# Compressed keys of the NSA group in four column blocks of the array, and S5 products of two parities written alternately

## The chip, the cores and the metric

The kernel runs on one core of one Trainium2 chip. The metric is the time of one execution on the device in microseconds (us); the time before is the median of three runs. Engines are named as in the profile: PE is the matrix engine, PEld its weight load, DVE the vector engine, ACT the scalar engine, POOL GpSimd, SP the engine whose queue issues most of the transfers.

## The reference

Two layers of a hybrid decoder trunk for 256 tokens of width 2048, in f32. Each layer has a token-mixing block and a gated MLP of inner width 5632; both stand between two RMS norms and are shifted, scaled and gated by a vector that is computed from `c` (adaLN, a 2048 x 12288 product per layer). The mixing block projects the tokens once, hands the columns to four groups, and projects the joined results back:

```python
proj = h @ w_in
o_a = mla_mixer(...)    # multi-head latent attention, 4 heads
o_b = s5_mixer(...)     # diagonal complex state space model, 32 groups of 64 states
o_c = nsa_mixer(...)    # compressed, selected and windowed attention
o_d = gdn_mixer(...)    # gated delta rule, 4 heads, chunks of 64 tokens
o = concatenate([rms_norm(o_a), rms_norm(o_b), rms_norm(o_c), o_d])
return o @ w_out
```

Two pieces of it are touched by the change. In the NSA group the keys (and likewise the values) of overlapping blocks of 32 tokens, one block every 16 tokens, are flattened and sent through a small MLP:

```python
h = gelu((xb + pos_emb).reshape(B, N, 32 * 128) @ w1)    # 15 blocks, w1: 4096 x 128
return h @ w2
```

In S5 the input is mapped to complex states, scanned over time, and mapped back: `bu = u B`, `x_t = lam x_(t-1) + bu_t`, `y = Re(C x) + D u`, then gelu and a gated linear unit.

## The kernel before

**The stream.** All large products run on weights that pass once through the chip. A tile of 128 x 1024 f32 (512 KB) is loaded by SP's queue (`wload`), ACT rounds it to a first part `wh` (line 366), DVE subtracts to get the rest `wl` (line 367), and PE makes three products of the parts of weights and activations for each product wanted (`mm3`); their results lie in four PSUM tiles named `mm`. In the trace these are the products whose name begins with `mm<-`, here called the products of the stream; their operands are `ht` (activations) with `wh` or `wl`. The adaLN products of later blocks run in the background on tiles `rawa`, on DVE (line 412).

**The mixers.** Beside the stream stand the products of the groups. They are f32, and PE makes two passes for each, so that one product of the program shows as two records of the trace. Their results lie in PSUM tiles `mx`, in two pools `mx0` and `mx1` of two tiles each; `self.lane` says which of them a part of the program draws on, and `None` lets it draw on both in turn (lines 133 to 138). `mixers` (line 1423) issues in this order: S5 (on `mx0`), the narrow columns, the compression of the NSA keys and values (`nsa_compress`, on `mx1`), the two halves of GDN (two heads each; half 0 on `mx0`, half 1 on `mx1`), MLA (`mx0`), the NSA attention (`mx1`, later both), the output gate. `project_out` follows with the `w_out` weights.

**Who sets the order.** The program is issued once, and the framework's scheduler lays out from it, at build time, a fixed order of instructions for each engine, from dependences, buffers, priorities and its own estimates of time. On PE it puts the products of the groups between those of the stream. Each engine then runs its list in order. A part of a group that waits for another engine has products of the stream put before it, as long as there are any whose weights and PSUM tile are to be had: the stream's products are what PE does while a chain of small steps runs on ACT and DVE.

**NSA compression.** `st` holds the tokens by their place q in a stride of 16, `[128 features, 16, 18]`: 16 strides, and two columns for the position embedding. For each q one product of weights `st[:, q]` (18 columns) with 256 columns of `w1` is added to `acc[:18]`; `w1` comes in four transfers to tiles `rawm`, four q in each. `acc` is copied to `ab`, turned by two transposes (`tp`) to `psT`, and the small MLP goes on from there. All this happens twice per layer, for keys and values.

**S5.** Pairs of groups lie in eight quads; a pair has a parity `par`, which is the half of the 128 rows on which its input lies (rows 0 to 63 or 64 to 127). For each half of the quads and each parity, in turn: eight products V (64 rows deep, 128 columns, one PSUM tile for the real and one for the imaginary part), some twenty steps on DVE (rotate, scan, rotate back), then twelve products y, which write the 64 output partitions of the parity, then four gelus. The DVE steps leave the states in `t1`, `t2`, which the products y read. The tables of S5 (`s5_tables`, line 1280) are made in the time before; the products of its taps write 64 partitions of the output for either parity `e`.

**GDN and MLA.** A half of GDN begins on PE with the decay products (`mx<-tri,gg`), goes through normed keys to an inverse by blocks of 32 x 32, and ends with the state update over four chunks. MLA begins with two norms, and then its up-projections, `mx<-arena,rawm` 128x256.

Of the kernel before, what the change touches and what calls it, by code (L numbers as in the profile page):

```python
# [16 lines left out]
AF = mybir.ActivationFunctionType  # L17
# [26 lines left out]
RSC = -8192.0        # factor that rsqrt_cols leaves on its result  # L44

MBOOST = 300        # the same of the mixers' own weights
BOOST = 2500        # how far ahead of the arithmetic the weight stream is scheduled

# arena map (floats per partition)
A_KVT = 0                           # token-major narrow columns  # L50
A_SIL0 = A_KVT + 1704               # GDN inputs of heads 0, 1
A_GA = A_SIL0 + 1536                # S5, then GDN heads 0, 1, then MLA
A_SIL1 = A_GA + 6160                # S5 tables; GDN inputs of heads 2, 3
A_GB = A_SIL1 + 1536                # S5 tables; GDN heads 2, 3, then NSA
A_OT = A_GB + 7168                  # mixer outputs, feature-major
A_KEEP = A_OT + 4096                # compressed keys and values of the NSA group
NA = A_KEEP + 1024
A_X = A_KVT                         # the residual stream, but for the time of the mixers
A_Z = A_X + 4096                    # output of the mixing block before its norm
A_GP = A_SIL1                       # the output gate of the mixing block  # L60
FIRST = (O_U, O_U + 256, O_GQ)      # columns of the first products
A_TAB = A_SIL1                      # S5 tables, the rotations last
A_ROT = A_TAB + 4608
A_SCR, N_SCR = A_OT + 2048, 3072    # S5 tables being built
A_GPF = A_SCR                       # the output gate of the FFN
AT = [A_ROT + g * 1024 for g in range(4)] + [A_Z + g * 1024 for g in range(5)] + [A_OT, A_OT + 1024]   # the FFN's inner activations
ADA_DVE = (0, 2, 4, 6, 9, 11)       # tiles of a quarter that DVE multiplies
# [6 lines left out]
class Region:  # L74
    """Sequential carving of a range of the arena."""
# [16 lines left out]
class Ker:  # L92
    def __init__(self, ctx, tc, I, out):
# [5 lines left out]
        # operands in two parts of half the mantissa: h^T; then the mixer outputs, or the FFN's activations  # L99
# [11 lines left out]
        self.lane = None                # which of them the current group of instructions draws on; None: both in turn  # L111
# [4 lines left out]
        self.side = iter(())             # work between the tiles of the weight stream, one step at each  # L116
# [8 lines left out]
    # ---------------------------------------------------------------- helpers  # L125
# [20 lines left out]
    def rsqrt(self, v, y, a):  # L146
        """y = v ** -0.5; v and a are overwritten."""
# [9 lines left out]
    def rsqrt_cols(self, ss):  # L157
        """RSC * (ss / D + EPS) ** -0.5 of a few columns, in fewer dependent steps than rsqrt."""
# [26 lines left out]
    def sincos(self, ang, sin, cos, t):  # L185
        """sin and cos of ang; cos and t double as scratch."""
        nc = self.nc
        self.reduce_2pi(ang, cos, t)
        nc.scalar.activation(sin, cos, AF.Sin)
        nc.vector.scalar_tensor_tensor(t, cos, -1.0, cos, op0=ALU.mult, op1=ALU.max)  # L190
        nc.vector.tensor_scalar(t, t, -1.0, math.pi / 2, op0=ALU.mult, op1=ALU.add)
        nc.scalar.activation(cos, t, AF.Sin)

    # -------------------------------------------------------------- constants
    def constants(self):
# [39 lines left out]
        # compressed-block masks: valid where t >= 16 n + 31  # L235
# [26 lines left out]
    def condition(self):  # L262
        """silu(c), one column of 128 features each."""
# [12 lines left out]
    def vectors_ada(self, l, rg):  # L276
        """Per-feature vectors of the modulation, one column of 128 features each."""
# [10 lines left out]
    def vectors(self, l, rg):  # L288
        """Per-feature vectors of the rest."""
# [40 lines left out]
        # column 0: dt_bias, column 1: a_log  # L330
# [12 lines left out]
    # --------------------------------------------------------------- streams  # L343
    def wload(self, parts):
        """parts: list of (view of the raw tile, source AP); one raw tile of up to 1024 columns."""
# [18 lines left out]
    def split(self, src, hi, lo):  # L364
        """src in two parts of half the mantissa each, hi + lo."""
# [21 lines left out]
    def mm3(self, out, a, b, start, stop):  # L387
        """out (+)= a^T b with both in two parts."""
# [4 lines left out]
    def mload(self, parts):  # L393
        """Weights of the mixers, through a small ring of their own."""
# [6 lines left out]
    # ------------------------------------------------------------------ adaLN  # L401
# [24 lines left out]
        # the sum over partitions: within blocks of 32 by a transpose of the blocks, then over the four blocks  # L426
# [46 lines left out]
    def ada_out(self, l, b, cols, j=0):  # L473
        """Columns j and on of block b."""
# [18 lines left out]
    def gate_out(self, l, which):  # L493
        """gate * post-norm gain / RSC to DRAM, as one row."""
# [7 lines left out]
    def gate_rows(self, l, which):  # L502
        """That row, on all partitions."""
# [17 lines left out]
    def set_diag(self, ss):  # L521
        """diag takes the scale of the rows, from their sums of x^2, ss [128, 2]."""
# [6 lines left out]
    def pre_norm(self, l, which):  # L529
        """Fills h^T, 4 tiles of 4 chunks each; a generator that stops after each quarter of the features."""  # L530
# [27 lines left out]
    def norm_start(self, h):  # L558
        """Half of the features; the others along with the products."""
# [7 lines left out]
    def x_stats(self):  # L567
        """Row sums of x^2 [128, 2] from those of the blocks."""
# [8 lines left out]
    def post_block(self, ps, j, gp, sums, z, last, tts=(0, 1)):  # L577
        """One 512-column block of y (two PSUM tiles); z takes gate * y; sums the row sums of y^2, and of z^2 and 2 x z."""
# [15 lines left out]
    def residual(self, sums, zs, done):  # L594
        """x += r z, r the scale of the rows; the sums of the new x^2 as x^2 + r (2 x z + r z^2)."""
# [1132 lines left out]
```

## Time and profile before

| | us |
|---|---|
| median of three runs | 2695.22 (2687.34 to 2700.55) |
| span of the profiled execution | 2692.3 |
| left between that span and the median | 2.9 |

The trace is of one execution. A row with `xN` is N instructions in a row with the same form; the number behind the start is how long the whole run took, with the pipelined end of the last one, so the distance from a start to the next row's start is the better measure of what a run costs PE. `128*18 128x256` means weights of 128 rows and 18 columns, and 256 columns that stream past them on 128 rows. `[1.15 <-ACT arena L1280]` is idle time before a row and what ended it.

### The profile page before, as it was taken

What the parts mean: (1) busy time and instruction counts of PE and PEld (TensorE: products, weight loads), DVE (VectorE), ACT (ScalarE), POOL (GpSimd) and SP (SyncE); (2) the same over time, 40 slices, a digit from 0 to 9 for tenths busy, and PEclk for the clock granted to TensorE, in tenths of its full rate; (3) what the DMA queues carried; (4) which work ended last, traced back from release to release, by engine and by line L of the source; (5) the groups of instructions that cost most, each with busy time, mean ns of one, the idle gap of its engine ahead of it and who ended that gap; (6) DMA issues with size and microseconds to landing.
All of it is one profiled execution on the core that took longest, in us unless ns stands there. A gap on an engine that the chain in (4) does not pass through costs nothing. (4 is left out here: it accounts for less than half of the span.)

```text
span 2692.3 us, 44696 instructions
## 1 busy us (share of the span) xinstructions
PE 2553.3 (95%) x17587; PEld 2257.8 (84%) x17587; DVE 1924.8 (71%) x3036; ACT 1260.7 (47%) x2025; POOL 9.6 (0%) x21
## 2 busy tenths in 40 slices
PE   5899999798999999999998999999899999999998
PEld 2478788687999999988877879888799999998886
DVE  6668888778877777776878888865677655555555
ACT  4244554546545444444545445555544444444443
POOL 0000000000000000000000000000000000000000
PEclk7889999899999999999999999999999999999999
DMA  8986887676888888877776667835588766665554
GB/s 269 298 242 188 259 277 226 202 268 217 274 287 277 283 286 284 293 247 234 232 255 228 189 201 243 267 123 170 180 272 280 224 187 188 183 186 188 188 188 148
DMA packets 325899, 621.43 MB, mean 231 GB/s; under 512 B 45132, under 2 KB 131640, under 8 KB 324152
## 3 DMA queue, kind: packets, MB, share of 16 engines
q1 hardware_dynamic: 317632, 617.36, 71.5%
q8 instruction: 138, 2.26, 0.3%
q10 hardware_dynamic: 8056, 1.21, 0.3%
q14 instruction: 73, 0.60, 0.1%
HBM read 614.26 MB, written 4.23 MB: 230 GB/s over the span
## 5 line engine op out<-in xcount | busy, mean ns | idle before, releaser
L127 PE MATMUL mm<-ht,wh 128*128 128x256 f32 x7232 | 1311.4, 283 | 2.9 <-ACT wh L366 2.9
L366 ACT CAST wh<-raw 128x1024 fp32r<-128x1024 f32 (+1 forms) x740 | 771.2, 1043 | 953.8 <-PE mm L127 751.2
L367 DVE TENSOR_TENSOR wl<-raw,wh 128x1024 fp32r<-128x1024 f32 (+1 forms) x740 | 893.2, 1213 | 346.1 <-ACT wh L366 344.2
L127 PEld LDWEIGHTS mm<-ht,wh 128*128 128x128 f32 x7232 | 1114.1, 189 | 15.2 <-issue 6.8
L127 PE MATMUL mm<-ht,wl 128*128 128x256 f32 x3616 | 1023.9, 283 | 7.9 <-DVE wl L367 7.6
L127 PEld LDWEIGHTS mm<-ht,wl 128*128 128x128 f32 x3616 | 681.7, 189 | 20.2 <-DVE wl L367 12.8
L412 DVE SCALAR_TENSOR_TENSOR acc<-rawa,condc,acc 128x1024 f32<-128x1024 f32 x310 | 397.3, 1282 | 216.5 <-DMA rawa<-in_w_ada_dram 215.0
L127 PE MATMUL mm<-wh,ht 128*128 128x512 f32 (+1 forms) x1600 | 507.4, 395 | 3.4 <-ACT ht L366 2.9
L127 PEld LDWEIGHTS mm<-wh,ht 128*128 128x128 f32 x1600 | 300.9, 189 | 68.0 <-ACT ht L366 3.2
L127 PE MATMUL mm<-wl,ht 128*128 128x512 f32 (+1 forms) x800 | 316.1, 395 | 1.7 <-DVE wl L367 1.7
L127 PE MATMUL mx<-wh,ht 128*128 128x512 f32 x704 | 221.4, 395 | 0.0
L127 PE MATMUL mx<-arena 128*128 128x128 f32 (+8 forms) x1432 | 199.1, 280 | 12.5 <-ACT arena L1417 4.7
L127 PEld LDWEIGHTS mx<-arena 128*128 128x128 f32 (+5 forms) x1432 | 156.0, 170 | 51.4 <-issue 20.2
L127 PEld LDWEIGHTS mm<-wl,ht 128*128 128x128 f32 x800 | 151.6, 190 | 34.0 <-DVE wl L367 3.0
L127 PEld LDWEIGHTS mx<-wh,ht 128*128 128x128 f32 x704 | 132.0, 187 | 32.1
L127 PE MATMUL mx<-wl,ht 128*128 128x512 f32 x352 | 139.3, 396 | 0.9 <-DVE wl L367 0.8
L131 PE MATMUL mx<-ident,arena 128*128 128x128 f32 (+3 forms) x367 | 68.4, 290 | 32.4 <-ACT arena L1280 11.0
L367 DVE TENSOR_TENSOR ht<-arena,ht 128x1024 fp32r<-128x1024 f32 x52 | 63.6, 1223 | 39.4 <-ACT ht L366 39.0
L131 PEld LDWEIGHTS mx<-ident,arena 128*128 128x128 f32 (+3 forms) x367 | 44.4, 148 | 53.7 <-ACT arena L1280 12.7
L1557 DVE SCALAR_TENSOR_TENSOR arena<-mm,v,arena 128x255 f32<-128x255 f32 (+1 forms) x176 | 78.2, 476 | 4.3 <-ACT arena L1555 3.5
L127 PEld LDWEIGHTS mx<-wl,ht 128*128 128x128 f32 x352 | 66.0, 187 | 18.1 <-DVE wl L367 2.1
L366 ACT CAST ht<-arena 128x1024 fp32r<-128x1024 f32 x52 | 54.2, 1050 | 56.5 <-PE mm L127 32.3
(308 smaller groups left out, 1514.1 us busy)
## 6 DMA issues: line engine op xcount, KB each, us to landing
raw<-in_ffn_w_in_dram SPq DMA_DIRECT2D x352, 512.0 KB
rawa<-in_w_ada_dram SPq DMA_DIRECT2D x348, 512.0 KB
raw<-in_ffn_w_out_dram SPq DMA_DIRECT2D x176, 512.0 KB
raw<-in_w_in_dram SPq DMA_DIRECT2D x116, 512.0 KB
raw<-in_w_out_dram SPq DMA_DIRECT2D x64, 512.0 KB
rawm<-in_w_ada_dram SPq DMA_DIRECT2D x28, 512.0 KB
raw<-in_w_in_dram SPq DMA_DIRECT2D x16, 426.0 KB
raw<-in_w_in_dram SPq DMA_DIRECT2D x16, 354.0 KB
```

Of the source, the lines that this page charges most:

```text
L127: self.nc.tensor.matmul(out, lhsT=lhsT, rhs=rhs, start=start, stop=stop)
L131: self.nc.tensor.transpose(out, in_, self.ident[:k, :k])
L366: self.nc.scalar.copy(hi.bitcast(F32R), src)
L367: self.nc.vector.tensor_sub(lo.bitcast(F32R), src, hi)
L412: self.last_mac = self.nc.vector.scalar_tensor_tensor(acc, w, self.condc[:, kc:kc + 1], acc, op0=ALU.mult, op1=ALU.add)
L1557: nc.vector.scalar_tensor_tensor(c[:, s:], ps[m][:, :256 - s], self.fconv(l, 2 - s, f), c[:, s:], op0=ALU.mult, op1=ALU.add)
```

## The change

It has three parts.

1. `nsa_compress`: `st` has 32 columns for each q instead of 18, zeroed by POOL first. The four q of a `rawm` tile go to four blocks of 32 output partitions, `acc[32q : 32q + 32]`, each with its own sum over the four tiles. All 128 partitions are copied to `ab`. Instead of two transposes, four products with columns of `ident2` (two identities of 64, one above the other) turn `ab` and add the four blocks.
2. `s5_tables`: the loops over the parity `e` and over real and imaginary part are swapped.
3. `s5`: the products V of both parities come first, then the DVE steps of one parity and of the other, with a second pair of buffers `t1`, `t2` in the place of MLA's outputs, then the products y of both parities, written alternately. In `mixers`, S5 draws on all four `mx` tiles (`lane = None`).

```diff
-            st = r(16, 18)
+            st = r(16, 32)
+            nc.gpsimd.memset(st, 0.0)
...
-                    self.mm(acc[:18], st[:, q0 + q], raw[:, q * 256:(q + 1) * 256], q0 + q == 0, q0 + q == 15)
-            ab = r(256)[:18]
-            nc.scalar.copy(ab, acc[:18])
+                    self.mm(acc[32 * q:32 * q + 32], st[:, q0 + q], raw[:, q * 256:(q + 1) * 256], q0 == 0, q0 == 12)
+            ab = r(256)
+            nc.scalar.copy(ab, acc)
             psT = self.mx()
             for i in range(2):
-                self.tp(psT[:, i * 32:i * 32 + 18], ab[:, i * P:(i + 1) * P])
+                for j in range(2):
+                    self.mm(psT[:, i * 32:i * 32 + 32], ab[:, i * P:(i + 1) * P], self.ident2[:, 32 * j:32 * j + 32], j == 0, j == 1)
...
             for qd in range(4):
-                for e in range(2):
-                    for ri in range(2):
+                for ri in range(2):
+                    for e in range(2):
...
-        for qr in range(4):
-            half, par = qr // 2, qr % 2
+        for half in range(2):
             quads = range(4 * half, 4 * half + 4)
...
+            V = [[view(self.mx()) for _ in range(2)] for _ in range(2)]
             for ri in range(2):
-                ps = self.mx().rearrange("p (e n) -> p e n", e=4)
                 for e, qd in enumerate(quads):
-                    self.mm(ps[:, e], G[o:o + 64, qd, ri], Uc[o:o + 64, qd], True, True)
-                V.append(ps)
+                    for par in range(2):
+                        o = 64 * par
+                        self.mm(V[par][ri][:, e], G[o:o + 64, qd, ri], Uc[o:o + 64, qd], True, True)
...
+            y = [view(self.mx()) for _ in range(2)]
             for e, qd in enumerate(quads):
-                yy = y[o:o + 64, e]
-                self.mm(yy, To[o:o + 64, qd], Uc[o:o + 64, qd], True, False)
-                for ri, t in enumerate((t1, t2)):
-                    self.mm(yy, H[:, 2 * qd + par, ri], t[:, e, 0:P], False, ri == 1)
+                for par in range(2):
+                    o = 64 * par
+                    self.mm(y[par][o:o + 64, e], To[o:o + 64, qd], Uc[o:o + 64, qd], True, False)
+                for ri in range(2):
+                    for par in range(2):
+                        o = 64 * par
+                        self.mm(y[par][o:o + 64, e], H[:, 2 * qd + par, ri], ts[par][ri][:, e, 0:P], False, ri == 1)
...
+        self.lane = None
+        self.s5(l, r5, Uc, oT["s5"])
         self.lane = 0
-        self.s5(l, r5, Uc, oT["s5"])
```

The scheduler makes its order anew, and three places of PE's list in layer 0 show what comes of it. In each row the name left of the arrow is the tile written, with its number; the shape is that of the result, partitions by columns; `xN` is N products of the program in a row.

First the beginning of S5's first products V. Before, the tiles `mx0_1283` and `mx0_1288` are the real and imaginary part of parity 0:

```order
L127 MATMUL mx0_1283<-arena_58 128x128 x2
L127 MATMUL mx0_1288<-arena_58 128x128 x2
L127 MATMUL mm_1533<-wh_1540,ht_59 128x426
L127 MATMUL mx0_1283<-arena_58 128x128
L127 MATMUL mx0_1288<-arena_58 128x128
L127 MATMUL mm_1533<-wl_1541,ht_59 128x426
L127 MATMUL mm_1533<-wh_1540,ht_59 128x426 x2
```

In the changed kernel `mx1_1285` and `mx0_1286` belong to parity 0, `mx1_1287` and `mx0_1288` to parity 1:

```order
L127 MATMUL mx1_1285<-arena_58 128x128
L127 MATMUL mx1_1287<-arena_58 128x128
L127 MATMUL mx1_1285<-arena_58 128x128
L127 MATMUL mx1_1287<-arena_58 128x128
L127 MATMUL mx0_1286<-arena_58 128x128
L127 MATMUL mx1_1285<-arena_58 128x128
L127 MATMUL mx0_1288<-arena_58 128x128
L127 MATMUL mx0_1286<-arena_58 128x128
L127 MATMUL mx0_1288<-arena_58 128x128
L127 MATMUL mx0_1286<-arena_58 128x128
```

Products of the two parities, which use different rows of the array, now stand partly next to each other: four such pairs are in this piece, and 14 of the 32 that there could be in both layers. The others follow one of their own parity, or stand alone.

Second, the products y. Before, one parity's last ten of twelve:

```order
L127 MATMUL mm_1694<-wh_1851,ht_59 128x426
L127 MATMUL mm_1694<-wl_1852,ht_59 128x426
L127 MATMUL mm_1694<-wh_1851,ht_59 128x426
L127 MATMUL mx0_1360<-arena_58 64x128 x10
L127 MATMUL mm_1693<-wh_1851,ht_59 128x426
L127 MATMUL mm_1693<-wl_1852,ht_59 128x426
L127 MATMUL mm_1693<-wh_1851,ht_59 128x426
```

In the changed kernel, the last ten of the second parity in the second half of the quads (those of the first, `mx1_1439`, stand in the same way 51 rows earlier):

```order
L127 MATMUL mm_2204<-ht_59,wh_2240 128x256 x2
L127 MATMUL mm_2204<-ht_59,wl_2241 128x256
L127 MATMUL mm_2204<-ht_59,wh_2240 128x256 x2
L127 MATMUL mx0_1440<-arena_58 64x128 x10
L127 MATMUL mm_2204<-ht_59,wl_2241 128x256
L127 MATMUL mm_2204<-ht_59,wh_2240 128x256 x2
L127 MATMUL mm_2204<-ht_59,wl_2241 128x256
```

The twelve products of a parity still stand as one, one and ten to the same tile, in all eight places of both layers; no two of different parities stand next to each other within the ten.

Third, the beginning of GDN's half 1, `mx1<-tri,gg6`. Before, the products of the stream around it are of `w_in` (`mm<-ht,wh`, 128x256):

```order
L127 MATMUL mm_4564<-ht_59,wh_4633 128x256 x2
L127 MATMUL mm_4564<-ht_59,wl_4634 128x256
L127 MATMUL mm_4564<-ht_59,wh_4633 128x256
L131 MATMUL mx1_3194<-ident_105,arena_58 128x128
L127 MATMUL mx1_3200<-tri_130,gg6_1875 128x128
L127 LDWEIGHTS identb_114
```

In the changed kernel those around it are already of `w_out` (`mm<-wh,ht`, 128x512):

```order
L127 MATMUL mm_4869<-wh_4877,ht_59 128x512
L127 MATMUL mm_4869<-wl_4878,ht_59 128x512
L127 MATMUL mm_4869<-wh_4877,ht_59 128x512
L131 MATMUL mx1_3202<-ident_105,arena_58 128x128
L127 MATMUL mm_4868<-wh_4877,ht_59 128x512
L131 MATMUL mx1_3202<-ident_105,arena_58 128x128 x2
L127 MATMUL mx1_3208<-tri_130,gg6_1877 128x128
L127 LDWEIGHTS identb_114
```

In PE's list of layer 0, up to this row, the changed kernel has 134 more products of the stream of 256 columns and 7 more of 512 than the kernel before. Between this row and the first up-projection of MLA there stood 156 products of the stream, and 41 now; that up-projection now stands in the middle of half 1's blocks of 32 x 32, and stood at half 1's end before. At the start of NSA's last norm of the layer 6 more products of the stream are behind. In layer 1 half 1 and MLA move the other way: 43 and 76 products of the stream earlier.

## Rows read from the trace of the kernel before

**Rows 1.** The page, head and part 1: busy us, share of the span, instructions.

```profile
span 2692.3 us, 44696 instructions
PE 2553.3 (95%) x17587; PEld 2257.8 (84%) x17587; DVE 1924.8 (71%) x3036; ACT 1260.7 (47%) x2025; POOL 9.6 (0%) x21
```

**Rows 2.** The page, costliest groups: count, busy us, mean ns, idle before and its releaser.

```profile
L366 ACT CAST wh<-raw 128x1024 fp32r<-128x1024 f32 (+1 forms) x740 | 771.2, 1043 | 953.8 <-PE mm L127 751.2
```

**Rows 3.** Groups by line and shape: NSA products, their weight loads, S5's V products.

```profile
L127 PE MATMUL mx<-rawm,arena 128*18 128x256 f32 x128 | 30.4, 380 | 3.8 <-DMA rawm<-in_nsa_w_v_dram 3.8
L127 PEld LDWEIGHTS mx<-rawm,arena 128*18 128x18 f32 x128 | 11.3, 97 | 17.5 <-DMA rawm<-in_nsa_w_v_dram 3.8 <-issue 1.5
L127 PE MATMUL mx<-arena 64*128 64x128 f32 x128 | 21.0, 302 | 5.6 <-ACT arena L1417 4.7 <-ACT arena L1390 0.6
```

**Rows 4.** Timeline of PE around NSA products: start us, us, instructions xcount.

```profile
285.84 0.40 PE L127 MATMUL mm<-ht,wh 128*128 128x256 f32 x2
286.07 0.28 PE L127 MATMUL mm<-ht,wl 128*128 128x256 f32 x1
286.20 0.28 PE L127 MATMUL mm<-ht,wh 128*128 128x256 f32 x1
286.40 3.63 PE L127 MATMUL mx<-rawm,arena 128*18 128x256 f32 x16
289.96 0.38 PE L127 MATMUL mm<-ht,wh 128*128 128x256 f32 x1
290.30 0.61 PE L127 MATMUL mx<-ident,ry 128*128 128x128 f32 x4
290.74 0.29 PE L127 MATMUL mx<-gg,tri 128*128 128x8 f32 x2
```

**Rows 5.** Timeline of PE: column blocks of the modulation and of the S5 taps.

```profile
36.30 1.02 PE L127 MATMUL mx<-raw,condc 128*1 128x512 f32 x4
37.21 1.03 PE L127 MATMUL mx<-rawm,condc 128*1 128x512 f32 x4
...
41.40 1.15 PE L127 MATMUL mx<-arena 128*64 128x64 f32 x30 [0.85 <-ACT arena L1280]
42.48 0.69 PE L131 MATMUL mx<-ident,arena 64*128 64x64 f32 x4
```

**Rows 6.** Timeline of PE: V products of S5, then y products.

```profile
180.05 1.16 PE L127 MATMUL mx<-arena 64*128 64x128 f32 x8
181.14 0.46 PE L127 MATMUL mm<-wl,ht 128*128 128x426 f32 x1
...
190.88 3.25 PE L127 MATMUL mx<-arena 128*64 128x128 f32 x20
```

**Rows 7.** Busy us of each engine (instructions) in stretches, granted clock, DMA share, GB/s.

```profile
381.00:415.00 34.00, 32.36 (x189) 27.57 (x188) 27.49 (x64) 17.54 (x34) 0.00 (x0) 1.00 0.91 288
415.00:461.00 46.00, 45.03 (x407) 40.62 (x406) 38.41 (x72) 22.15 (x47) 0.00 (x0) 1.00 0.71 222
462.00:541.00 79.00, 62.87 (x346) 50.23 (x346) 56.42 (x155) 38.82 (x106) 0.00 (x0) 0.91 0.63 198
1606.00:1736.00 130.00, 125.72 (x987) 114.02 (x988) 106.84 (x205) 71.57 (x155) 0.52 (x1) 1.00 0.82 258
```

**Rows 8.** Timeline of PE: first decay and first 32x32 products of GDN's halves, layer 0.

```profile
334.69 0.39 PE L127 MATMUL mx<-tri,gg 128*128 128x128 f32 x2
...
372.15 0.59 PE L127 MATMUL mx<-arena 32*32 32x32 f32 x16
...
415.22 0.39 PE L127 MATMUL mx<-tri,gg 128*128 128x128 f32 x2
...
452.38 0.59 PE L127 MATMUL mx<-arena 32*32 32x32 f32 x16
```

**Rows 9.** Timeline of PE: MLA's first up-projection; last products of the NSA attention.

```profile
462.38 1.03 PE L127 MATMUL mx<-arena,rawm 128*128 128x256 f32 x4
...
541.25 1.51 PE L127 MATMUL mx<-arena 128*128 128x128 f32 x12
```

More of the change, by code (lines that the diff above doesn't have):

```diff
@@ L878, in nsa_compress @@
                 for q in range(4):
-                    self.mm(acc[:18], st[:, q0 + q], raw[:, q * 256:(q + 1) * 256], q0 + q == 0, q0 + q == 15)
-            ab = r(256)[:18]
-            nc.scalar.copy(ab, acc[:18])
+                    self.mm(acc[32 * q:32 * q + 32], st[:, q0 + q], raw[:, q * 256:(q + 1) * 256], q0 == 0, q0 == 12)
+            ab = r(256)
+            nc.scalar.copy(ab, acc)
             psT = self.mx()
             for i in range(2):
-                self.tp(psT[:, i * 32:i * 32 + 18], ab[:, i * P:(i + 1) * P])
+                for j in range(2):
+                    self.mm(psT[:, i * 32:i * 32 + 32], ab[:, i * P:(i + 1) * P], self.ident2[:, 32 * j:32 * j + 32],
+                            j == 0, j == 1)
             a = r(2, 18)
@@ L1341, in s5 @@
         wz = r(2056)
-        t1, t2 = (wz[:, i * 516:(i + 1) * 516].rearrange("p (e n) -> p e n", e=4) for i in range(2))
+        wt = (wz, self.reg(A_OT + 1024, 1032)(1032))
+        ts = [[w[:, i * 516:(i + 1) * 516].rearrange("p (e n) -> p e n", e=4) for i in range(2)] for w in wt]
         zr, zi = (wz[:, 1032 + i * 512:1032 + (i + 1) * 512].rearrange("p (e n) -> p e n", e=4) for i in range(2))
@@ L1347, in s5 @@
         nc.sync.dma_start(glu, I["s5_w_glu"][l].rearrange("(k p) n -> p k n", p=P))
-        a1, a2 = t1[:, :, 1:], t2[:, :, 1:]
-        for t in (t1, t2):
+        for t in itertools.chain(*ts):
             nc.gpsimd.memset(t[:, :, 0:1], 0.0)
-        for qr in range(4):
-            half, par = qr // 2, qr % 2
+        view = lambda ps: ps.rearrange("p (e n) -> p e n", e=4)
+        for half in range(2):
             quads = range(4 * half, 4 * half + 4)
-            o = 64 * par
-            es = slice(8 * half + par, 8 * half + 8, 2)
-            Er, Ei = E[:, 0, es], E[:, 1, es]
-            V = []
+            V = [[view(self.mx()) for _ in range(2)] for _ in range(2)]
@@ L1359, in s5 @@
             for ri in range(2):
-                ps = self.mx().rearrange("p (e n) -> p e n", e=4)
                 for e, qd in enumerate(quads):
-                    self.mm(ps[:, e], G[o:o + 64, qd, ri], Uc[o:o + 64, qd], True, True)
-                V.append(ps)
-            TTm(a1, V[0], Er, mul)
-            TTm(a2, V[1], Ei, mul)
-            TTm(zr, a1, a2, add)
-            TTm(a1, V[1], Er, mul)
-            TTm(a2, V[0], Ei, mul)
-            TTm(zi, a1, a2, sub)
-            for z in (zr, zi):
-                for e, qd in enumerate(quads):
-                    d0 = self.s5m2[:, l, 2 * qd + par:2 * qd + par + 1].to_broadcast([P, P])
-                    nc.vector.tensor_tensor_scan(z[:, e], d0, z[:, e], 0.0, mul, add)
@@ L1375, in s5 @@
-            TTm(a1, zr, Er, mul)
-            TTm(a2, zi, Ei, mul)
-            TTm(a1, a1, a2, sub)
-            TTm(zr, zr, Ei, mul)
-            TTm(zi, zi, Er, mul)
-            TTm(a2, zr, zi, add)
-            y = self.mx().rearrange("p (q n) -> p q n", q=4)
-            for e, qd in enumerate(quads):
-                yy = y[o:o + 64, e]
-                self.mm(yy, To[o:o + 64, qd], Uc[o:o + 64, qd], True, False)
-                for ri, t in enumerate((t1, t2)):
-                    self.mm(yy, H[:, 2 * qd + par, ri], t[:, e, 0:P], False, ri == 1)
@@ L1387, in s5 @@
-            for h in range(2):
-                for s in range(2):
-                    of = 64 * h + 32 * par
-                    nc.scalar.activation(yv[of:of + 32, 2 * half:2 * half + 2, :, s], y[o + 32 * s:o + 32 * s + 32, h::2],
-                                         AF.Gelu_apprx_tanh)
+                    for par in range(2):
+                        o = 64 * par
+                        self.mm(V[par][ri][:, e], G[o:o + 64, qd, ri], Uc[o:o + 64, qd], True, True)
+            for par in range(2):
+                es = slice(8 * half + par, 8 * half + 8, 2)
+                Er, Ei = E[:, 0, es], E[:, 1, es]
+                Vr, Vi = V[par]
+                a1, a2 = (t[:, :, 1:] for t in ts[par])
+                TTm(a1, Vr, Er, mul)
+                TTm(a2, Vi, Ei, mul)
+                TTm(zr, a1, a2, add)
+                TTm(a1, Vi, Er, mul)
+                TTm(a2, Vr, Ei, mul)
+                TTm(zi, a1, a2, sub)
+                for z in (zr, zi):
+                    for e, qd in enumerate(quads):
+                        d0 = self.s5m2[:, l, 2 * qd + par:2 * qd + par + 1].to_broadcast([P, P])
+                        nc.vector.tensor_tensor_scan(z[:, e], d0, z[:, e], 0.0, mul, add)
+                TTm(a1, zr, Er, mul)
+                TTm(a2, zi, Ei, mul)
+                TTm(a1, a1, a2, sub)
+                TTm(zr, zr, Ei, mul)
+                TTm(zi, zi, Er, mul)
+                TTm(a2, zr, zi, add)
@@ new lines, in s5 @@
+            y = [view(self.mx()) for _ in range(2)]
+            for e, qd in enumerate(quads):
+                for par in range(2):
+                    o = 64 * par
+                    self.mm(y[par][o:o + 64, e], To[o:o + 64, qd], Uc[o:o + 64, qd], True, False)
+                for ri in range(2):
+                    for par in range(2):
+                        o = 64 * par
+                        self.mm(y[par][o:o + 64, e], H[:, 2 * qd + par, ri], ts[par][ri][:, e, 0:P], False, ri == 1)
@@ L1392, in s5 @@
+            for par in range(2):
+                o = 64 * par
+                for h in range(2):
+                    for s in range(2):
+                        of = 64 * h + 32 * par
+                        nc.scalar.activation(yv[of:of + 32, 2 * half:2 * half + 2, :, s],
+                                             y[par][o + 32 * s:o + 32 * s + 32, h::2], AF.Gelu_apprx_tanh)
         yg = Uc.rearrange("p q m -> p (q m)").rearrange("p (c t) -> p c t", c=4)
```

## Prediction

> **What bounds the kernel now.** I read the busy shares first. PE is busy for 2553.3 of 2692.3 us [rows 1]; no other engine comes near. The group of ACT's casts shows the same from the other side: ACT is idle for 953.8 us ahead of them, and 751.2 of these end with a product of the stream [rows 2], so weights lie ready and PE is late. Where PE is full, a microsecond of its work that goes is a microsecond of time. So the second question is where it is full, and that is read from the busy time by stretches, in the mixers, since the change touches nothing else. In 415 to 461 us PE has 45.0 of 46 us, in layer 1 from 1606 to 1736 it has 125.7 of 130. But from 462 to 541 us, the end of layer 0's mixers, it has 62.9 of 79 at a granted clock of 0.91 [rows 7]: there the chain of MLA and NSA sets the time, and 16 us of PE go unused. What comes before that stretch is worth something only as far as it lets MLA begin earlier. The third view is the timeline of PE around the products that change, for their price and for signs that blocks of the array work side by side.
>
> **NSA compression.** Both layers have 128 records of this form, busy 30.4 us in all [rows 3]. In the timeline 16 of them start at 286.40 and the next row at 289.96 [rows 4]: 3.56 us, 0.2225 each, so 28.5 us for all. The new products have 32 columns and the same 256 that stream past, so one alone should cost as much. How many run at once, no row of before shows for four blocks. Two blocks are shown: the modulation's products alternate between output rows 0 and 32, four records of 512 columns in 0.91 us (36.30 to 37.21) [rows 5], 0.2275 each, where twice a record of 256 would be 0.445. That is two at a time, to 2%. From below, four blocks that work like two give half, 14.2 us; from above, all four at once a quarter, 7.1 us. I take the quarter, since the two blocks lose almost nothing to each other: minus 21.4 us.
>
> Their weights come four times as dense as before, and a load takes 97 ns by its mean [rows 3]. That is no time of occupation: the taps are 30 records with as many loads of 64 columns in 1.08 us (41.40 to 42.48) [rows 5], 0.036 each for load and product together. Eight loads of 32 columns then fit into 0.29 us, and the eight records of a `rawm` tile need 0.445. The Trainium skill ("TensorEngine Tiling (Array Packing)", section "Restrictions") says that column tiling disables the fast weight load; if these loads were one after another at their mean, the form would cost 128 x 0.097 = 12.4 us rather than 7.1, and the sum below would be 5.3 us smaller. The taps' row speaks against it, for 64 columns.
>
> The four blocks must be summed. Four transposes per layer become eight products, two records each, so 16 records more in both layers; four records with an identity take 0.44 us (290.30 to 290.74) [rows 4], so plus 1.8 us. The copy of `ab` and the zeroing of `st` lie on ACT and POOL, whose busy shares are 47% and below 1% [rows 1]; they are some 0.5 us longer in a chain with hundreds of stream products behind it. Cost zero; if that cover were gone, 2 us for four names. The waits for the `rawm` tiles are 3.8 us for 128 records [rows 3], and stay. NSA: minus 19.6 us, from minus 12.4 (two at a time) to minus 21.4.
>
> **S5.** Eight records V take 1.09 us (180.05 to 181.14) [rows 6]. Row halves with the same columns occur nowhere before, so the bounds are nothing and half the time. In the order of the changed kernel 14 pairs of products stand next to each other; each pair that overlaps in full saves two records, 0.27 us: 3.8 us at most. Since I have no row, I take half: minus 1.9 us. The products y have the larger price, 3.25 us for 20 records [rows 6], and blocks of columns as the modulation's. But in the order the twelve of a parity stand together in all eight places: parity 0 is ready some twenty DVE steps before parity 1, and the scheduler doesn't hold it back. So nothing is saved, and that part of the change doesn't do what it says. The taps' loop: a record of 128 columns takes 1.09 / 8 = 0.136 us here, one of 64 alone about half, 0.068; the taps' 0.036 [rows 5] is half of that again, so the old order already runs two at a time. Zero; bounds plus and minus 0.5 us.
>
> The work taken from PE is 21.5 us, 10.8 in each layer.
>
> **What layer 0 gives back.** The order also moves GDN's half 1 behind 134 products of 256 columns and 7 of 512. A product of 256 costs 0.12 us (three from 285.84 to 286.20) [rows 4], one of 512 about twice that: 16.1 + 1.7 = 17.8 us. The half's decay, at 415.22 before [rows 8], comes at 415.2 - 10.8 + 17.8 = 422.2. From decay to the blocks of 32 x 32 it was 37.5 us in half 0 and 37.2 in half 1 [rows 8], although PE had different products to fill in; I take this for the chain's length: 459.4. MLA's first up-projection now stands among these blocks, so it comes at about 460, and came at 462.38 [rows 9]: 2.4 us won, not 10.8. Behind it the chain of 79 us is as before; the rest of half 1, 8.6 us before (452.38 to about 461), runs alongside, in the 16 us that PE had free. At the end 6 products of 512 more are done, 1.4 us. Layer 0: minus 3.8 us, I say minus 4. One end: the chain is shorter than 37 us when PE has little else (it was busy for 45.0 of 46 then), and MLA comes 10.8 early: minus 11. The other: the rest of half 1 delays MLA's chain by all of its 8.6 us: plus 5.
>
> In layer 1 half 1 and MLA move forward, with more products left to cover them, and PE is full: minus 10, from minus 7 to minus 11.
>
> **Sum.** Minus 14 us on the span of 2692.3. That span lies 2.9 us below the median of the runs, and I leave these alone: 2695.2 - 14 = 2681 us. By the ends of the two layers the forecast's own range is 2673 to 2693.
>
> **Rivals.**
> - *All of it is kept.* If half 1's chain goes faster uncovered, both layers gain their 10.8 us: 2674. For it: PE's list is fuller than 95% in that stretch, so the chain's own steps on PE stood behind stream products. Against it: the two halves' 37 us agree to 0.3.
> - *The four blocks run two at a time*, or their weights set the pace. Then NSA gives 12.4 instead of 19.6, 3.6 less per layer; layer 0 falls from 4 to about 0 and layer 1 from 10 to 6: 2689, no change that can be told. For it: only pairs are shown. Against it: nothing in the pair's row says that a second partner would be refused.
> - *Cover is moved and nothing saved: slower.* If the blocks of columns take turns, PE's work stays, plus 1.8 us. Half 1's decay comes at 415.2 + 17.8 = 433.0, its blocks of 32 x 32 at 470.2, MLA 7.8 later than before, and with the rest of half 1 in its way up to 16.4; PE would stand idle that much longer, at the lower clock of such stretches. Less the 1.4 us: plus 14 or so, 2709. It decides from the point where NSA saves under some 7 us of PE per layer while half 1 and MLA run one after the other. For it: the order is as it is, and products of the stream that ran beside half 1 are gone when it starts. Against it: the modulation's pair.
> - *DMA takes the place of PE.* In 381 to 415 us the transfers are busy for 0.91 at 288 GB/s [rows 7]; PE faster by a tenth there would meet them. That costs layer 0 a few us that it mostly doesn't keep anyway; it is within the forecast.
>
> **How the numbers follow.** A measurement of this kernel can tell 0.5%, 13.5 us: below 2681.7 is faster, above 2708.7 slower. Forecast 0.50, its middle almost on the lower bound, so I give faster 0.26 of it and same 0.24. All kept 0.20, faster. Two at a time 0.17, same. Slower rival 0.10. The remaining 0.03 is a shift of the order elsewhere, spread over all three. Faster 0.47, same 0.42, slower 0.11. The range goes from 2663 (all kept, V's full 3.8 us, and a measurement as far below the middle as the lowest of before, 2687.34) to 2702, short of the slow rival.
>
> **What would show it.** In the trace after: four `rawm` products of 32 columns should start within a few ns of each other, and a tile's eight records take 0.45 us (0.9 would be two at a time, 1.78 none). V's alternating pairs either start together or 0.11 to 0.14 us apart. The y runs of 20 records should still take 3.2 us. Half 1's decay should come near 422 us, MLA's up-projection near 460, and the end of layer 0's mixers at 537 to 541; PE's idle time between the decay and the up-projection should be some 8 us more. Layer 1's mixers should be 10 us shorter. I am wrong if layer 0's mixers end before 532 or after 546, if layer 1's keep their length, or if the FFN, which the change leaves alone, is where the difference lies.

## The result

The changed kernel takes 2707.1 us in the median of 12 runs (2688.15 to 2717.04), the kernel before 2691.2 in 12 (2682.72 to 2700.55): a ratio of 1.0057, 95% interval 1.0037 to 1.0077. It is slower by 15 us, where 14 us faster was forecast, and lies outside the range.

The head of the changed kernel's page (compare [rows 1]):

```profile
span 2703.5 us, 44772 instructions
PE 2549.7 (94%) x17611; PEld 2262.6 (84%) x17611; DVE 1927.9 (71%) x3036; ACT 1260.8 (47%) x2024; POOL 11.9 (0%) x29
```

Its groups by line and shape, NSA's products and S5's V (compare [rows 3]):

```profile
L127 PE MATMUL mx<-rawm,arena 128*32 128x256 f32 x128 | 9.4, 387 | 1.9 <-DMA rawm<-in_nsa_w_v_dram 1.2 <-DMA rawm<-in_nsa_w_k_dram 0.7
...
L127 PE MATMUL mx<-arena 64*128 64x128 f32 x128 | 21.8, 351 | 5.4 <-ACT arena L1428 5.1 <-ACT arena L1401 0.2
```

The NSA products fell from 30.4 to 9.4 us, as forecast, but PE's whole busy time fell by 3.6 only. The rest came back elsewhere as slower work (the granted clock over the whole span is 0.969, and was 0.978), and the time without work grew by 15 us. The timeline of PE shows the three kinds of products that changed:

```profile
199.06 3.25 PE L127 MATMUL mx<-arena 128*64 128x128 f32 x20
...
205.59 2.11 PE L127 MATMUL mx<-arena 64*128 64x128 f32 x24
207.63 0.47 PE L127 MATMUL mm<-wh,ht 128*128 128x426 f32 x1
...
276.37 1.07 PE L127 MATMUL mx<-rawm,arena 128*32 128x256 f32 x16
277.37 0.50 PE L127 MATMUL mm<-ht,wh 128*128 128x256 f32 x2
```

Sixteen NSA records take 1.00 us (276.37 to 277.37), 3.56 before [rows 4]: all four blocks run at once. The 24 V records, 16 of them alternating, take 2.04 us; at 0.11 each, the distance between those that don't alternate, it would be 2.7. The y run is unchanged at 3.25 [rows 6].

Layer 0's mixers in PE's timeline: half 1's decay, MLA's first up-projection, the half's blocks of 32 x 32, and the last causal mask of the NSA attention, first after and then before (compare [rows 8, 9]):

```profile
431.31 0.39 PE L127 MATMUL mx<-tri,gg 128*128 128x128 f32 x2
...
468.78 0.60 PE L127 MATMUL mx<-arena,rawm 128*128 128x256 f32 x2
469.31 0.59 PE L127 MATMUL mx<-arena 32*32 32x32 f32 x16
...
552.72 0.22 PE L127 MATMUL mx<-cmask,identb 128*128 128x128 bf16 x1
```

```profile
535.46 0.22 PE L127 MATMUL mx<-cmask,identb 128*128 128x128 bf16 x1
```

Decay and 32 x 32 are 38.0 us apart, as forecast. MLA came 6.4 us later than before, the last mask 17.3. An end of layer 0's mixers after 546 us was named in the prediction as a sign of being wrong.

Between decay and mask lies the hand-over from half 1 to the NSA attention: the last step of the half (`on`, on DVE), then the first copy of NSA's turned queries (`qT`, on ACT), after and before:

```profile
488.72 0.74 DVE L1161 SCALAR_TENSOR_TENSOR arena<-arena,v,mx 128x512 f32<-128x512 f32 x1
494.87 0.58 ACT L923 COPY arena<-mx 128x512 f32<-128x512 f32 x1
```

```profile
473.52 0.74 DVE L1157 SCALAR_TENSOR_TENSOR arena<-arena,v,mx 128x512 f32<-128x512 f32 x1
474.81 0.59 ACT L919 COPY arena<-mx 128x512 f32<-128x512 f32 x1 [2.47 <-PE mx L131]
```

So half 1 ends 58 and 59 us behind its decay, after MLA's first up-projection in both kernels, and NSA begins behind it. The busy times of this stretch, decay to last mask, after and before (us, then PE, PEld, DVE, ACT, POOL busy, granted clock, DMA share, GB/s):

```profile
431.31:552.72 121.41, 96.25 (x597) 78.24 (x595) 86.98 (x214) 50.53 (x133) 0.00 (x0) 0.85 0.59 184
```

```profile
415.22:535.46 120.24, 103.14 (x725) 87.00 (x724) 92.69 (x219) 55.50 (x138) 0.00 (x0) 0.94 0.66 206
```

It is as long as before, with 128 PE records fewer in it: what PE did beside it went ahead of it, and PE idles and runs at the lower clock here. PE's waits there name the softmax of the attention (line 740). DVE, which does a part of each softmax, waits for the tiles of the adaLN product in the background (line 412), and runs its list in order. Waited us, times and longest, from 405 to 557 us after, and from 400 to 545 before:

```profile
PE mx L131 <- ACT arena L740: 17.5, 4, 6.0
DVE acc L412 <- DMA rawa<-in_w_ada_dram: 20.2, 20, 2.2
```

```profile
PE mx L131 <- ACT arena L740: 8.1, 3, 5.7
DVE acc L412 <- DMA rawa<-in_w_ada_dram: 7.6, 7, 1.9
```

The second place is the beginning of S5 in layer 1: 40 us from 6 us before its first V, after and before, in the same columns:

```profile
1487.80:1527.80 40.00, 37.38 (x170) 31.42 (x171) 30.59 (x52) 12.62 (x27) 0.00 (x0) 0.79 0.61 192
```

```profile
1472.50:1512.50 40.00, 37.45 (x196) 31.79 (x197) 36.33 (x61) 16.43 (x34) 0.00 (x0) 0.91 0.75 223
```

PE is as busy, and does 26 records less, at a granted clock of 0.79 for 0.91.

### The profile page after: what moved, and what is told of

Its sections match the earlier page's. It is cut to its first block, busy times and chain, and to the rows that moved or that the text cites. A ratio compares the mean times of both kernels' runs of the same rounds, so it can differ in the third digit from the quotient of the medians.

```text
span 2703.5 us, 44772 instructions
## 1 busy us (share of the span) xinstructions
PE 2549.7 (94%) x17611; PEld 2262.6 (84%) x17611; DVE 1927.9 (71%) x3036; ACT 1260.8 (47%) x2024; POOL 11.9 (0%) x29
## 4 chain that ended last, share of the span: by engine, by line
PE 66%; DMA 10%; DVE 8%; issue 3%; ACT 2%; SPq 0%; DVEq 0%; ACTq 0%
PE mm L127 51%; PE mx L127 13%; DMA rawa<-in_w_ada_dram 10%; DVE wl L367 3%; DVE acc L412 2%; PE mx L131 1%; ACT wh L366 1%; DMA rawm<-in_nsa_w_v_dram 0%; DVE arena L1569 0%; SPq L349 0%; DMA rawm<-in_s_c_im_dram 0%; ACT rawm L1284 0%; DVE arena L1343 0%; DVE arena L1629 0%; ACT junk L575 0%
## 5 line engine op out<-in xcount | busy, mean ns | idle before, releaser
L127 PE MATMUL mm<-wh,ht 128*128 128x512 f32 (+1 forms) x1600 | 516.4, 400 | 5.5 <-ACT ht L366 4.9
L127 PE MATMUL mx<-arena 128*128 128x128 f32 (+8 forms) x1432 | 205.4, 291 | 15.2 <-ACT arena L1428 5.1
```

The costliest lines, as they stand in the source:

```text
L127: self.nc.tensor.matmul(out, lhsT=lhsT, rhs=rhs, start=start, stop=stop)
```

## The experiments

Two theories were formed on these rows. A: the place of GDN's half 1 in the order sets the end of layer 0's mixers, and its shift costs more than the products save. B: the rearranged S5 loses time at its start. C laid 4 us at the start of the program to the taps. The runs were made in three sessions, in which the kernel before had medians of 2690.7 to 2696.8 us; so the ratio to it, given behind each time with its interval, compares better than the time. First each part alone:

**nsa_only**, part 1.

> Part 1 alone (NSA in four column blocks). In PE's list GDN's half 1 of layer 0 then stands behind 1508 products of the stream (1354 before, 1495 with all three parts), MLA's up-projection behind 1536. Theory A (the part saves its 20 us of PE work, and the new order of layer 0's end costs as much or more): no faster than before, 2685 to 2705, with layer 0's mixers ending some 10 us or more later than before. Theory B (the loss is S5's): about 2676, the saving in full in both layers. Theory C (the loss of 4 us at the start is the taps'): the first V of S5 at 162.6 us as before.

Measured: 2716.8 us, ratio 1.0066 (1.0046 to 1.0087). The part with all of the saving is as slow as the whole change. Decay, MLA, last mask:

```profile
426.03 0.39 PE L127 MATMUL mx<-tri,gg 128*128 128x128 f32 x2
...
461.84 0.60 PE L127 MATMUL mx<-arena,rawm 128*128 128x256 f32 x2
...
547.48 0.22 PE L127 MATMUL mx<-cmask,identb 128*128 128x128 bf16 x1
```

MLA stands where it stood before (462.38), and the end is 12 us later: the end goes with half 1 (10.8 later), not with MLA. Counted from first V, half 1 is 6.5 later, MLA 4.9 earlier, the last mask 7.7 later. B as the cause of the whole loss falls too: S5 is as before here, and the saving doesn't come. The first V came at 166.93, without the taps' change, so C falls; it came at 164.8 to 168.5 in all other profiles, and 162.6 belongs to the one execution of before.

**s5_only**, part 3.

> Part 3 alone (S5 rearranged, on all four mx tiles). Half 1 of layer 0 then stands behind 1256 products, MLA behind 1427, so earlier than before. Theory A: layer 0's end is covered better, so same or faster, 2680 to 2693. Theory B (PE waits at S5's start and runs there at the lower clock): slower by some 10 us, 2700, with more time at the lower clock around the first V in both layers.

Measured: 2696.5 us, 0.9998 (0.9979 to 1.0017). Both theories are half right. Layer 0, with half 1 early, is 9 us shorter from first V to the norm of the FFN; layer 1's S5 starts at the lower clock, and the layer is 4.5 us longer:

```profile
1466.90:1506.90 40.00, 37.30 (x162) 31.14 (x163) 29.12 (x51) 11.79 (x25) 0.00 (x0) 0.74 0.61 186
```

**taps_only**, part 2.

> Part 2 alone (loops of the taps swapped). The order of the mixers is that of before. Theory C: the first V of S5 comes 4 us later, and the whole is 4 us slower, 2695. Theories A and B: the same as before, 2691.

Measured: 2698.2 us, 1.0002 (0.9988 to 1.0017). Nothing, as forecast. From first V to the next norm its layers take 471.5 and 442.4 us, before's 471.9 and 445.3; PE's order in the mixers is the same, and so it shows how well two executions of one order agree.

**all_gdn300**, all parts, GDN at a higher priority:

```diff
+            q_ = qkv(hp)
+            with self.tc.high_priority(300):
-                self.gdn_half(l, hp, ..., qkv(hp), G, on[hp])
+                self.gdn_half(l, hp, ..., q_, G, on[hp])
```

> All three parts, and GDN's halves scheduled with a priority 300 steps higher, which puts layer 0's half 1 behind 1407 products of the stream instead of 1495, and MLA's up-projection behind 1507 instead of 1536, close to before (1354 and 1510). Theory A: layer 0's mixers end 10 to 17 us earlier than in the changed kernel, and the whole is faster than before, 2675 to 2688. Theories B and C: the loss stays, 2700 to 2707.

Measured: 2697.9 us, 1.0004 (0.9989 to 1.0019). By the ratios the same products at another place win back 14 us of 15: A for layer 0, whose last mask comes 22.7 us earlier from first V than in the changed kernel. But it isn't faster than before, which A expected too.

The next four move half 1 by itself. The hold is one line around the last products of `w_in`, the mark the first decay product:

```diff
-            ps = self.gemm_b(W, O_GZ + hp * 256)
+            with self.after(self.mark):
+                ps = self.gemm_b(W, O_GZ + hp * 256)
```

**nsa_hold.**

> Part 1 alone, and the products of the output gate (192 of the stream, the last of w_in) held behind the decay of GDN's half 1. Half 1 of layer 0 then stands behind 1296 products of the stream (1508 in part 1 alone, 1354 before), MLA's up-projection behind 1475 (1536, 1510). Theory A (the saving of part 1 is real, and the place of half 1 ate it): 2673 to 2686, 30 us faster than part 1 alone. Rival D (PE's time is not the price of the NSA products, so nothing is to be had from them): 2690 to 2697, as before.

Measured: 2709.0 us, 1.0055 (1.0034 to 1.0075). Missed by both: A promised 2686 at most, D 2697.

**before_hold.**

> The kernel before with the same hold (half 1 behind 1296, MLA behind 1475), nothing of the change. It is the control of the run with part 1 and the hold. Theory A: the hold alone is worth 0 to 6 us (2688 to 2694), and part 1 behind it 10 to 19 us. If the hold alone gives 10 us or more, the place of half 1 is worth that, and part 1 little.

Measured: 2709.8 us, 1.0075 (1.0059 to 1.0090). The hold itself costs 20 us, where A gave it a gain of 0 to 6, so these two tell little of part 1: 0.2% between them. From decay to last mask it is 127 us with the hold, 7 more than else, and half 1's decay came no earlier than in all_gdn300. A number of products ahead in the order is not a time.

**all_hold.**

> All three parts and the hold (half 1 behind 1296, MLA behind 1475, as in the run of part 1 with the hold). Theory A alone: as that run, or a us or two faster by V's pairs. Theory B in its smaller form (S5 rearranged makes PE run its first V products of layer 1 at the lower clock, some 13 us more of it): 4 to 8 us slower than part 1 with the hold, 2680 to 2691.

Measured: 2714.9 us, 1.0079 (1.0050 to 1.0108). 6 us above nsa_hold, within the intervals of both: inconclusive by time, though its S5 start has the clock of 0.74. The forecast of 2691 at most fell with nsa_hold's.

**before_late**, nothing of the change, `high_priority(-300)` around the halves.

> The kernel before with nothing saved, GDN's halves at a priority 300 steps lower: half 1 of layer 0 behind 1507 products of the stream (1508 in part 1 alone), MLA's up-projection behind 1532. Theory A: the place alone costs 15 to 30 us, 2706 to 2722, with PE's idle time in layer 0's mixers 12 us or more above before's. If it costs under 5 us, the place is not the cause.

Measured: 2762.6 us, 1.0278 (1.0257 to 1.0298). Larger than forecast: this order also put the half's second part behind MLA, so that the half ends 98.7 us behind its decay. Decay, MLA, last mask:

```profile
434.45 0.27 PE L127 MATMUL mx<-tri,gg 128*128 128x128 f32 x1
...
464.71 0.38 PE L127 MATMUL mx<-arena,rawm 128*128 128x256 f32 x1
...
585.85 0.22 PE L127 MATMUL mx<-cmask,identb 128*128 128x128 bf16 x1
```

MLA is in its place again, and the mixers end 50 us later. The last four ask for a version that keeps the saving. `lane = None` around the old S5 gives another order in layer 1, a priority of 2600 in layer 0 brings half 1 forward there.

**nsa_lane.**

> Part 1 with S5 as before on all four mx tiles, no priority: half 1 of layer 0 behind 1496 products, layer 1 in the order of nsa_lane_gdn. Theory A2: layer 0's mixers 10 us or more longer than in nsa_lane_gdn, layer 1's equal to that run's: 2684 to 2698.

Measured: 2714.7 us, 1.0060 (1.0039 to 1.0081), above the forecast. Decay 428.85, MLA 463.91, last mask 547.99.

**nsa_lane_gdn.**

> Part 1 with S5 as before but on all four mx tiles, and GDN's halves of layer 0 at a priority 2600 steps higher: half 1 of layer 0 behind 1312 products of the stream, in layer 1 behind 7969. Theory A2 (layer 0's mixers end some 120 us after half 1's decay, whatever stands beside; part 1's saving in layer 1 is taken back by the lower clock that S5 rearranged brings): half 1's decay 250 us or less after S5's first V (264 in the changed kernel), layer 1's mixers 433 to 437 us from its first V to the next layer norm (441 in the changed kernel, 442 to 445 before), and 2672 to 2684 in all. Rival D (nothing is to be had from the NSA products): 2690 to 2700.

Measured: 2697.9 us, 1.0002 (0.9980 to 1.0023): rival D's range, not A2's. Against nsa_lane, layer 0's half 1 is 11.7 us earlier from first V, MLA 0.8 later, the end 12.5 earlier:

```profile
419.11 0.27 PE L127 MATMUL mx<-tri,gg 128*128 128x128 f32 x1
...
466.77 1.03 PE L127 MATMUL mx<-arena,rawm 128*128 128x256 f32 x4
...
537.51 0.22 PE L127 MATMUL mx<-cmask,identb 128*128 128x128 bf16 x1
```

Layer 1 missed its forecast of 433 to 437 us: 453, with the old S5 on four tiles at a clock of 0.74 as well. But nsa_lane, whose instructions on PE stand in the same order in layer 1, took 445.7 us there, at 0.91: the order alone does not fix the clock.

**lane_gdn**, the control.

> The control of the run nsa_lane_gdn: the same without part 1 (half 1 of layer 0 behind 1335 products, in layer 1 behind 7890). Theory A2: 9 to 20 us slower than that run, near before, 2688 to 2698. If it is as fast, what is won there comes from the priority and the tiles.

Measured: 2700.2 us, 1.0012 (0.9996 to 1.0028). Only 2 us above nsa_lane_gdn: of 18 us of PE's work that part 1 takes away, nothing that can be told arrives in this pair. The expectation of 9 to 20 us fell.

**all_gdn**, all parts, priority in layer 0 alone.

> All three parts and the same priority in layer 0 alone (half 1 of layer 0 behind 1336 products; layer 1 in the order of the changed kernel). Theory A2: layer 0's mixers as in the run nsa_lane_gdn, layer 1's 5 us or more longer, with 20 us or more at the lower clock (5 to 11 us in kernels with the old S5): 2680 to 2692. If S5's rearrangement costs nothing, as nsa_lane_gdn.

Measured: 2690.6 us, 0.9969 (0.9953 to 0.9985): by the ratio 8 us faster than before (6 by the medians), and below the changed kernel's ratio by 0.9%. It is the best version tried. The clock at layer 1's S5 is 0.79, as forecast, but its layer 1 is shorter than that of nsa_lane_gdn, not longer:

```profile
1471.40:1511.40 40.00, 37.76 (x171) 31.51 (x171) 30.80 (x53) 12.32 (x26) 0.00 (x0) 0.79 0.62 192
```

All profiles side by side, in us, one execution each. V is the start of S5's first product, "norm" that of the next norm's first product (`mx<-diag`); the clock is that of 40 us from 6 us before layer 1's V. The profile of nsa_lane_gdn is of an execution 16 us above its median, that of nsa_hold of one 11 us below; the others lie within 4 us. The stretch from layer 0's norm to layer 1's V, which no edit touches, takes 837 to 853 us in them, so a few us in one row mean little.

| run | L0: V to decay | V to MLA | V to last mask | decay to last mask | L1: V to norm | clock at L1's S5 |
|---|---|---|---|---|---|---|
| before | 252.6 | 299.8 | 372.9 | 120.2 | 445.3 | 0.91 |
| taps_only | 253.7 | 300.8 | 372.1 | 118.4 | 442.4 | 0.96 |
| the change | 264.3 | 301.8 | 385.8 | 121.4 | 441.1 | 0.79 |
| nsa_only | 259.1 | 294.9 | 380.6 | 121.4 | 454.1 | 0.96 |
| s5_only | 231.2 | 281.3 | 364.1 | 132.9 | 449.8 | 0.74 |
| all_gdn300 | 244.1 | 284.0 | 363.1 | 119.0 | 447.2 | 0.79 |
| nsa_lane | 263.7 | 298.8 | 382.9 | 119.1 | 445.7 | 0.91 |
| nsa_lane_gdn | 252.0 | 299.6 | 370.4 | 118.4 | 453.2 | 0.74 |
| lane_gdn | 246.3 | 295.2 | 364.9 | 118.6 | 448.6 | 0.87 |
| all_gdn | 246.4 | 295.6 | 368.2 | 121.8 | 442.8 | 0.79 |
| nsa_hold | 244.6 | 296.0 | 371.6 | 127.0 | 447.8 | 0.96 |
| before_hold | 245.9 | 296.8 | 372.7 | 126.8 | 450.1 | 0.92 |
| all_hold | 252.7 | 303.5 | 379.2 | 126.5 | 453.1 | 0.74 |
| before_late | 269.4 | 299.7 | 420.8 | 151.4 | 477.5 | 0.96 |

## Why the prediction was wrong

**Right.** NSA's four blocks run at once and save 21 us. At 0.0625 us a record with its load the 128 cost 8.0 us, so loads one after another, 12.4 by the prediction's estimate, are not what the trace shows. The Trainium skill ("TensorEngine Tiling (Array Packing)", section "Restrictions") says that column tiling disables the fast weight load; whether it was off here, no run shows. Further, half 1's chain to the 32 x 32 blocks is 38.0 us, 37.2 forecast; the y products don't alternate; the taps are worth nothing. V's pairs start together: 21 of 26 pairs of records 6 or 7 ns apart, the others up to 34. At 0.11 us a record that is 2.9 us by an estimate, for 1.9 forecast; it is not to be had from V's group, part of which ran at the lower clock. One small term was short: the sums by `ident2` are 32 records of 4.1 us instead of 8 of 1.2, so 24 more and not 16, plus 2.9 for the 1.8 forecast.

**The step that failed** is the end of "What layer 0 gives back": MLA's first up-projection was taken for what the end hangs on, "Behind it the chain of 79 us is as before; the rest of half 1, 8.6 us before (452.38 to about 461), runs alongside, in the 16 us that PE had free." That rest was read too short: before, the half ends at 474.3 us, 22 behind its blocks of 32 x 32. And the table says otherwise. In nine of the fourteen profiles the last mask stands 118.4 to 121.8 us behind half 1's decay, while MLA comes anywhere from 35 to 49 us behind it. In five of the nine the mask also stands 70 to 73 us behind MLA, and either could bind; the other four, in which MLA is further ahead (the change, nsa_only, nsa_lane, all_gdn300), have 79 to 86, and there the end goes with half 1. In layer 0 of all fourteen profiles the first copy of NSA's turned queries comes from 0.3 us before to 6.4 us behind the end of half 1, also in before_late, where that end is 98.7 us behind the decay; the products that give the queries had been copied out 47 us or more before that. The NSA attention works in the arena region of half 1 (`A_GB`) and on its PSUM tiles (`mx1`), and in the program comes after it; that this and not something else binds them was read from the code, and no run tried a region of its own. Half 1's decay was forecast at 7.0 us later than before, MLA 2.4 earlier. By the decay, layer 0 would have been 7 us longer, and the forecast about 3 us faster, no change, not 14. The rule has its limit: with half 1 21 us earlier (s5_only) the last mask came only 9 us earlier, 132.9 behind the decay, and with the hold it is 127.

The decay came 11.7 later from first V (16.1 in absolute time, of which 4.4 are before V), for the 7.0: between V and decay PE was at the lower level of its clock for 17.1 us, before for 6.8. Ten more at half the speed are an estimate of 5 us, which is about the remainder. From the last mask to the norm another 4.1 us were lost, and PE has two waits there that the kernel before has not:

```profile
584.99 0.50 PE L127 MATMUL mm<-wh,ht 128*128 128x512 f32 x1 [3.29 <-ACT ht L366]
...
643.44 0.50 PE L127 MATMUL mm<-wl,ht 128*128 128x512 f32 x1 [2.98 <-DVE wl L367]
```

From V to norm layer 0 is 17.0 us longer, where minus 4 was forecast. The two profiles' spans differ by 11.2 us: 4.4 before V, 17.0 here, minus 6.1 from the norm to layer 1's V, which the change leaves alone, and minus 4.2 in layer 1.

**A term of the wrong size** is layer 1: minus 10 forecast, minus 4.2 measured against the profile of before, minus 1.3 against taps_only. Its premise, "PE is full", held; what it is full of changed. In the 40 us at S5's start PE has the same busy time and 26 records less than in before, 32 less than in taps_only. A clock of 0.79 means 17 of 40 us at the lower of the two levels, 0.91 means 7: ten us more at half speed are 5 us lost. Over the whole layer, from V to norm, it was 24.4 us at the lower level for 10.8, so 6.8 lost of the 10.8 that the products save: about 4 are left by this estimate, and 4.2 were measured. The rearranged S5 had the low clock at its start in all five kernels with it (0.74 to 0.79), the old one on one pool in none of six (0.91 to 0.96), the old one on four tiles between (0.74 to 0.91, both ends in one order). What the engine did there: V products of 64 rows, more of them at a time, with short waits for the gathers between; which of these lowers the clock stays open. It is not the only way to lose layer 1: nsa_only, at 0.96 there, took 454.1 us. Its half 1 came 5.9 later from V than before's, and the layer has 28.0 us without work on PE for 17.5 and 27.3 at the lower level for 10.8.

**Rivals.** The slower rival was the right sign with the wrong cause: it wanted blocks that take turns. Its other half, products of the stream that leave half 1 uncovered, is what happened, without the condition on the blocks. That its 2709 us lies so near the measured 2707.1 is luck: it had the decay at 433.0 with nothing saved, and the decay came at 431.3 with the products saved, 4.4 us lost before V and 5 to the clock. The 16 us that PE had free were no room: between decay and mask it had 128 records less to do, and idle time rose from 17.1 to 25.2 us.

**Open.** Part 1's 18 us could not be shown in a time. Its pairs, nsa_lane_gdn with lane_gdn and nsa_hold with before_hold, differ by 0.1 and 0.2%, where 18 us would be 0.7. In two more, nsa_only with before and the changed kernel with s5_only (the taps being worth nothing), the kernel with part 1 is the slower by 0.7 and 0.6%. Rival D of the expectations, that nothing is to be had from these products as the kernel stands, is not refuted. From V to last mask of both layers PE is without work for 42.6 us in nsa_lane_gdn and 29.6 in lane_gdn, which would be most of what the products gave; but the first is the profile that lies 16 us above its median. all_gdn's layer 1 is 10 us shorter than that of nsa_lane_gdn, and 7.5 of these lie between two executions of one order, nsa_lane and nsa_lane_gdn.

A rival for the length of 118 to 122 us stands untested. In each of the nine profiles 29 to 31 adaLN steps (line 412) lie between decay and mask on DVE, and 34 in the 132.9 us of s5_only. In the changed kernel DVE waits there for 16.9 us for their tiles, for 7.6 before, with steps of the softmax behind them in its list; and the profile's chain that ended last runs through these steps and transfers from 491 to 535 us. No run takes the background out, so how much of the stretch is half 1 and NSA and how much the pace of these tiles stays open.

## What to carry to other kernels

Where a scheduler lays out the order, a change's own saving is one term and the new order another, and the second can be the larger: look for the chain that the stage's end hangs on, follow every region and buffer that its last link shares, and price the shift of its first link, not of the link that waits in the profile of before. Here products saved beside a chain that didn't get shorter came back as idle time and a lower clock. The same three parts were worth minus 8 us with half 1 brought forward and plus 15 without.

## What the runs showed of the hardware

- Four column blocks of f32 products of 32 columns ran together: 16 records of 256 in 1.00 us, 0.0625 each, for 0.2225 one at a time. Two row halves with the same columns, into different PSUM tiles, start 6 or 7 ns apart in most pairs.
- PE's busy share does not show the clock: 37.4 of 40 us busy at 0.91 was 196 records, at 0.79 it was 170.
- One order of PE's instructions (layer 1 of nsa_lane and nsa_lane_gdn) ran its first 40 us at a granted clock of 0.91 in one execution and of 0.74 in the other, 190 records and 159, and the layer took 445.7 and 453.2 us.
